# A decoder layer on one Trainium2 core: auxiliary products pinned in VectorE's queue, a head with direct column transposes, and modulation halves added on ScalarE

## The chip, the cores and the metric

The kernel runs on one core of a Trainium2 chip. The metric is the device time of one execution in microseconds, the median of several. The core has a matrix engine (TensorE, PE in the profile, with PEld for its weight loads), VectorE (DVE), ScalarE (ACT), GpSimd (POOL) and a sync engine (SP) that issues nearly all DMAs here. Each engine takes its instructions in the order of its own queue and waits on semaphores for the others.

## The reference

One layer on 256 tokens with 2048 channels, in float32:

```python
mod = silu(c) @ w_mod + b_mod
sh1, sc1, g1, sh2, sc2, g2 = jnp.split(mod, 6, axis=-1)
h = _rms_norm(x, mix_norm_pre) * (1.0 + sc1) + sh1
y = _token_mixer(h, ...)       # h @ w_in, attention, gated linear attention, merge, w_out
x = x + g1 * _rms_norm(y, mix_norm_post)
h = _rms_norm(x, ffn_norm_pre) * (1.0 + sc2) + sh2
y = _conv_ffn(h, ...)          # h @ w_up, conv of width 3, silu(gate) * value, w_down
x = x + g2 * _rms_norm(y, ffn_norm_post)
```

`c` is one vector of 2048 values, `w_mod` has 2048 x 12288 entries; `_rms_norm` divides each token by its root mean square.

## The kernel before

All weights pass through the core once. A weight *item* is 128 rows x 2048 columns, cut into two *parts* of 128 x 1024 (512 KB). Every product keeps float32 accuracy by splitting both operands into a rounded high half and the rest: for a part, ACT casts `hi` from the loaded `raw` (L272), DVE subtracts `lo = raw - hi` (L276), and PE multiplies hi by h_hi, lo by h_hi and hi by h_lo (`mm3`, L292 to L294). In the stages that put 512 columns out, a part is 12 matmuls of 512 columns; in `half_mm` (L343) it is 8 pairs of a 512-column and a 256-column matmul.

The loop at L1175 goes over the parts: at step q SP issues the load of part q+3 (four `raw` buffers), ACT and DVE prepare part q (three `hi`, three `lo` buffers), and PE multiplies part q-3. The stages follow one another: wS (phase 1: attention q, k, v and a quarter of the values), wOG (phase 2: output gate), the forget columns, wQK, wV, wGB and wBB, wGA and wBA, wO, then twice wU and wD.

Beside the weights run 224 *auxiliary* loads of 128 x 1024. For 192 of them DVE makes a product with `cact`, the silu of c copied to all partitions, and sums along the row (`mod_proc`, L207): two halves give one column of `mod`, added up at L211. The other 32 (`bias_proc`, L226) add the shift's share of the attention projection. The first 64 are *early*: they give scale and shift for h, one column of 128 channels for each item of phases 1 and 2, and have four buffers; the rest share three, later two, buffers (`auxb`). `aux_step` (L1165) runs the products that are due by their `pos` and issues the next loads.

The order on PE and SP is that of the code. On DVE and ACT a scheduler sets it, by its own estimate of when operands are there, except in blocks marked `manual_schedule`, such as the head. So an L207 stands in DVE's queue where the scheduler put it.

The head (L131 to L175) builds `cact`: for each 128 values of c DVE scales the identity by them, and PE multiplies it by ones, so that they stand on all partitions (L136, L139); ACT copies them out of PSUM (L143). It also squares x (DVE one half at L147, ACT the other at L149), makes 1/rms, and transposes x by a matmul with a diagonal of 1/rms (L171), whose result ACT copies to `xnT` (L173). `make_h1` (L352) then forms the column factor `a` on DVE (L355), h_hi on ACT (L357) and h_lo on DVE (L358); in phase 2 `make_h2` (L362) overwrites them with the shifted h (L365, L297, L298). `evac_1` (L372) takes phase 1's eight PSUM banks out, those of the first token tile (t = 0) on ACT, those of the second on DVE.

Of the kernel before, what the change touches and what calls it, by code (L numbers as in the profile page):

```python
# [38 lines left out]
def block_kernel(ctx: ExitStack, tc: tile.TileContext, x, cvec, pos, idn, cst, vec, vec2, gmask,  # L39
# [90 lines left out]
    with tc.manual_schedule(engines={ET.DVE, ET.Activation}):  # L130
        nc.scalar.activation(ccol, ccol, AF.Silu)  # L131

        def c_diag(n):
            dg = t2k()
            for j in range(4):
                nc.vector.tensor_scalar(out=dg[:, j * P:(j + 1) * P], in0=ident, scalar1=ccol[:, 4 * n + j:4 * n + j + 1],  # L136
                                        scalar2=None, op0=ALU.mult)
            ps = bank(n)
            nc.tensor.matmul(out=ps, lhsT=ones[:, :P], rhs=dg, start=True, stop=True)  # L139
            return ps  # L140

        def c_copy(n, ps):
            nc.scalar.copy(cact[:, n * 512:(n + 1) * 512], ps)  # L143

        def sums(t):
            ssx = small(2, "ssx")
            nc.vector.scalar_tensor_tensor(out=junk[:, t, :HW], in0=xh[:, t, :HW], scalar=1.0, in1=xh[:, t, :HW],  # L147
                                           op0=ALU.mult, op1=ALU.mult, accum_out=ssx[:, 0:1])
            nc.scalar.activation(junk[:, t, HW:], xh[:, t, HW:], AF.Square, accum_out=ssx[:, 1:2])  # L149
            return ssx  # L150

        def scale(ssx):
            ssy = small(1, "ssy")
            nc.vector.tensor_tensor(ssy, ssx[:, 0:1], ssx[:, 1:2], op=ALU.add)
            return diag_of(rstd_of(ssy, 1, float(D)))

        cps = [c_diag(n) for n in range(3)]
        c_copy(0, cps[0])
        s0 = sums(0)
        cps.append(c_diag(3))  # L160
        c_copy(1, cps[1])
        c_copy(2, cps[2])
        dgs = [scale(s0)]
        s1 = sums(1)
        c_copy(3, cps[3])
        for t in range(2):
            for q in range(4):
                pt = bank((4, 5, 6, 7, 0, 1, 2, 3)[4 * t + q])
                for j in range(4):
                    c = 4 * q + j  # L170
                    nc.tensor.matmul(out=pt[:, j * P:(j + 1) * P], lhsT=xh[:, t, c * P:(c + 1) * P], rhs=dgs[t],  # L171
                                     start=True, stop=True)
                nc.scalar.copy(xnT[:, 4 * q:4 * q + 4, t * P:(t + 1) * P], pt.rearrange("p (c t) -> p c t", c=4))  # L173
# [1111 lines left out]
```

## Time and profile before

| | |
|---|---|
| median of 3 runs | 1598.68 us (1593.1 to 1600.93) |
| profiled execution | 1597.75 us, of which the span from the first to the last instruction is 1595.6 us |
| busy share of PE, DVE, ACT | 98%, 77%, 52% |
| mean granted TensorE clock | 0.997 |
| moved from HBM | 399.68 MB, 252 GB/s over the span |

Busy times are sums of instruction durations over the span; a matmul's end is modelled, so the distance between two starts says more on PE than its busy share. A wait is put down to the instruction that came last by the profile. Times of instructions are microseconds from the start of the span.

### The profile page before, as it was taken

To read this page: it belongs to the slowest core of one execution; us is meant where nothing else is said; L and a number is where in the kernel's file an instruction comes from. 1 tells how busy PE (TensorE), PEld (TensorE's weight loads), DVE (VectorE), ACT (ScalarE), POOL (GpSimd) and SP (SyncE) were. 2 spreads that over 40 slices of the span, in tenths; PEclk is the share of its full clock that TensorE was granted. 3 is DMA by queue.
4 is the path that set the end of the run, shared out by engine and by line. 5 is a ranking of instruction groups with operands and counts; after the bars stand their busy time and mean duration, and the time that the engine had idled before them with its cause. 6 is when DMAs were issued, how large, how long until landed. Compare 5 with 4: busy or idle time off the path is not lost.

```text
span 1595.6 us, 21287 instructions
## 1 busy us (share of the span) xinstructions
PE 1563.3 (98%) x7752; PEld 1293.2 (81%) x7752; DVE 1222.5 (77%) x1869; ACT 825.7 (52%) x1221; POOL 17.0 (1%) x35
## 2 busy tenths in 40 slices
PE   8999999999999999999999999999999999999997
PEld 6878888877767788777888888888778888888886
DVE  7999989968977778877778877777546777776446
ACT  5455565544477544443366555555335555555333
POOL 0000000000000000000000000000000000000001
PEclk9999999999999999999999999999999999999999
DMA  9999987877777799889935667677665555555554
GB/s 367 382 352 410 360 274 257 277 273 256 250 244 263 257 306 326 293 293 314 354 133 199 230 231 238 217 245 231 231 224 187 182 185 185 186 186 189 194 197 132
DMA packets 154841, 403.18 MB, mean 253 GB/s; under 512 B 12720, under 2 KB 70704, under 8 KB 154480
## 3 DMA queue, kind: packets, MB, share of 16 engines
q1 hardware_dynamic: 154736, 401.82, 72.9%
q8 instruction: 61, 1.00, 0.3%
q14 instruction: 44, 0.36, 0.1%
HBM read 399.68 MB, written 2.10 MB: 252 GB/s over the span
## 4 chain that ended last, share of the span: by engine, by line
PE 31%; DMA 22%; DVE 13%; issue 5%; ACT 2%; SPq 1%; POOL 0%; DVEq 0%; POOLq 0%; ACTq 0%
DMA aux<-in_wM_dram 21%; PE ps L343 16%; DVE lo L276 6%; PE ps L293 5%; PE ps L294 5%; PE ps L292 5%; DVE aux L207 2%; DMA raw<-in_wO_dram 1%; ACT hi L272 1%; SPq L251 0%; DVE aux L348 0%; DVE t2k L742 0%; DVE t2k L1093 0%; DVE y L1134 0%; SPq L253 0%
## 5 line engine op out<-in xcount | busy, mean ns | idle before, releaser
L272 ACT CAST hi<-raw 128x1024 fp32r<-128x1024 f32 x520 | 544.9, 1050 | 476.1 <-PE ps L294 366.9
L276 DVE TENSOR_TENSOR lo<-raw,hi 128x1024 fp32r<-128x1024 f32 x518 | 629.2, 1221 | 142.0 <-ACT hi L272 139.6
L343 PE MATMUL ps<-h,hi 128*128 128x512 f32 x1664 | 582.0, 398 | 1.0 <-DVE h L1051 1.0
L343 PE MATMUL ps<-h,lo 128*128 128x256 f32 x1664 | 451.0, 281 | 1.0 <-DVE lo L276 0.9
L343 PEld LDWEIGHTS ps<-h,hi 128*128 128x128 f32 x1664 | 306.4, 188 | 69.2 <-issue 1.3
L343 PEld LDWEIGHTS ps<-h,lo 128*128 128x128 f32 x1664 | 314.0, 189 | 13.8 <-DVE lo L276 4.4
L207 DVE SCALAR_TENSOR_TENSOR aux<-aux,cact 128x1024 f32<-128x1024 f32 x128 | 156.4, 1223 | 145.7 <-DMA aux<-in_wM_dram 145.6
L292 PE MATMUL ps<-hi,h 128*128 128x512 f32 x608 | 240.0, 395 | 1.6 <-ACT h L297 1.1
L293 PE MATMUL ps<-lo,h 128*128 128x512 f32 x608 | 237.4, 391 | 2.6 <-DVE lo L276 2.5
L294 PE MATMUL ps<-hi,h 128*128 128x512 f32 x608 | 237.1, 390 | 1.5 <-DVE h L298 0.8
L293 PEld LDWEIGHTS ps<-lo,h 128*128 128x128 f32 x608 | 114.2, 188 | 29.2 <-DVE lo L276 4.9
L294 PEld LDWEIGHTS ps<-hi,h 128*128 128x128 f32 x608 | 114.1, 188 | 26.9 <-DVE h L298 1.2
L292 PEld LDWEIGHTS ps<-hi,h 128*128 128x128 f32 x608 | 114.2, 188 | 26.7 <-ACT h L297 1.5
L293 PE MATMUL ps<-lo,act_ab 128*128 128x512 f32 x256 | 100.3, 392 | 2.2 <-DVE lo L276 2.2
L294 PE MATMUL ps<-hi,act_ab 128*128 128x512 f32 x256 | 99.7, 389 | 0.0
L292 PE MATMUL ps<-hi,act_ab 128*128 128x512 f32 x256 | 99.7, 389 | 0.0
L207 DVE SCALAR_TENSOR_TENSOR early<-early,cact 128x1024 f32<-128x1024 f32 x64 | 78.0, 1218 | 1.3 <-ACT cact L143 1.3
L347 ACT ACTIVATE aux<-ps 128x256 f32<-128x256 f32 x88 | 33.5, 380 | 75.4 <-PE ps L343 75.2
L1090 ACT ACTIVATE t2k<-aux,vc 128x256 f32<-128x256 f32 x88 | 52.8, 601 | 26.6 <-DVE aux L348 26.4
L348 DVE SCALAR_TENSOR_TENSOR aux<-ps,aux 128x256 f32<-128x256 f32 x88 | 37.0, 421 | 35.6 <-ACT aux L347 35.6
L293 PEld LDWEIGHTS ps<-lo,act_ab 128*128 128x128 f32 x256 | 48.0, 188 | 14.4 <-DVE lo L276 4.6
L292 PEld LDWEIGHTS ps<-hi,act_ab 128*128 128x128 f32 x256 | 48.0, 188 | 10.1
(270 smaller groups left out, 1614.2 us busy)
## 6 DMA issues: line engine op xcount, KB each, us to landing
raw<-in_wU_dram SPq DMA_DIRECT2D x176, 512.0 KB, 3.8
aux<-in_wM_dram SPq DMA_DIRECT2D x128, 512.0 KB, 6.0
raw<-in_wD_dram SPq DMA_DIRECT2D x88, 512.0 KB, 3.9
early<-in_wM_dram SPq DMA_DIRECT2D x64, 512.0 KB, 6.7
raw<-in_wS_dram SPq DMA_DIRECT2D x32, 512.0 KB, 6.4
raw<-in_wOG_dram SPq DMA_DIRECT2D x32, 512.0 KB, 7.0
aux<-in_wS_dram SPq DMA_DIRECT2D x32, 512.0 KB, 5.7
raw<-in_wQK_dram SPq DMA_DIRECT2D x32, 512.0 KB, 5.4
```

The lines of the kernel that those rows point to most:

```text
L207: nc.vector.scalar_tensor_tensor(out=raw, in0=raw, scalar=1.0, in1=cact[:, half * HW:(half + 1) * HW], op0=ALU.mult, op1=ALU.mult, accum_o ...
L272: nc.scalar.copy(hi[:, :w], raw)
L276: nc.vector.tensor_tensor(lo[:, :w], raw, hi[:, :w].bitcast(F32), op=ALU.subtract)
L292: nc.tensor.matmul(out=o, lhsT=lh, rhs=rh, start=start, stop=False)
L293: nc.tensor.matmul(out=o, lhsT=lh, rhs=rl, start=False, stop=False)
L294: nc.tensor.matmul(out=o, lhsT=ll, rhs=rh, start=False, stop=stop)
L343: nc.tensor.matmul(out=o, lhsT=w, rhs=m, start=c == 0 and o is ps, stop=c == nk - 1 and o is ps)
L347: nc.scalar.activation(o, ps[:, TOK:], AF.Copy, scale=scale)
L348: nc.vector.scalar_tensor_tensor(out=o, in0=ps[:, :TOK], scalar=scale, in1=o, op0=ALU.mult, op1=ALU.add)
L1090: nc.scalar.activation(z, u, AF.Identity, scale=w2, bias=vc2[:, W_CB + f:W_CB + f + 1])
```

## The change

Three edits. **Products.** Each auxiliary product after the 64 early ones is traced inside `tc.issue_after(...)`: it gets an ordering edge, without a semaphore, behind the subtraction L276 of part `lq + 3`, where `lq` is the step at which its load was issued. **Head.** `cact` comes from transposing each column of c, broadcast along 128 columns, so DVE's sixteen scaled identities and the ones go; the first token tile is still transposed against the diagonal, the second is scaled by DVE first and transposed against the identity; `vec` is loaded from ACT's queue; parts 0 and 1 are prepared inside the head; the first half item of phase 1 runs its twelve matmuls as four hi, four lo, four h_lo. **Adds.** For the columns of phases 1 and 2, ACT adds each half as it comes (`Identity` with a column as bias, in phase 1 also one as scale) where DVE had one addition at the end and one for the factor; and `evac_1` gives two more of its eight copies to ACT.

```diff
-    nc.sync.dma_start(out=ident, in_=idn)
     nc.sync.dma_start(out=ccol, in_=cvec)
+    nc.sync.dma_start(out=ident, in_=idn)
...
-    nc.sync.dma_start(out=vc, in_=vec)
...
+    nc.scalar.activation(ccol, ccol, AF.Silu)
+    nc.scalar.dma_start(out=vc, in_=vec)
+    for n in range(4):
+        ps = bank((2, 6, 3, 7)[n])
+        for j in range(4):
+            nc.tensor.transpose(ps[:, j * P:(j + 1) * P], ccol[:, 4 * n + j:4 * n + j + 1].to_broadcast([P, P]), ident)
+        cps.append(ps)
...
+    c_copy(0)
+    square_v(0, 0)
+    nc.scalar.activation(junk[:, 0, HW:], xh[:, 0, HW:], AF.Square, accum_out=ssx[0][:, 1:2])
+    for n in range(1, 4):
+        c_copy(n)
+    rs = rstd_x(0)
+    square_v(1, 0)
+    nc.scalar.activation(junk[:, 1, HW:], xh[:, 1, HW:], AF.Square, accum_out=ssx[1][:, 1:2])
+    dg0 = diag_of(rs)
+    rs = rstd_x(1)
+    for q in range(2):
+        xs = xh[:, 1, q * HW:(q + 1) * HW]
+        nc.vector.tensor_scalar(out=xs, in0=xs, scalar1=rs, scalar2=None, op0=ALU.mult)
+    bw = modc[:, 16:32]
+    nc.vector.scalar_tensor_tensor(out=bw, in0=vc[:, V_BMOD + 16:V_BMOD + 32], scalar=1.0,
+                                   in1=vc[:, V_PRE1:V_PRE1 + 16], op0=ALU.add, op1=ALU.mult)
+    def x_transposes(t, qs=range(4)):
...
+                if t == 0:
+                    nc.tensor.matmul(out=pt[:, j * P:(j + 1) * P], lhsT=xc, rhs=dg0, start=True, stop=True)
+                else:
+                    nc.tensor.transpose(pt[:, j * P:(j + 1) * P], xc, ident)
+            nc.scalar.copy(xnT[:, 4 * q:4 * q + 4, t * P:(t + 1) * P], pt.rearrange("p (c t) -> p c t", c=4))
...
+        if idx < 32:
+            c = idx % 16
+            w, b, o = (1.0, vc[:, V_BMOD + c:V_BMOD + c + 1], modc) if idx < 16 else (vc[:, V_PRE1 + c:V_PRE1 + c + 1], bw[:, c:c + 1], acol)
+            o = o[:, c:c + 1]
+            nc.scalar.activation(o, acc[:, half:half + 1], AF.Identity, scale=w, bias=o if half else b)
+            if half:
+                a["post"]()
+            return
...
-        a["raw"] = raw
+        a["raw"], a["lq"] = raw, S.get("q", 0)
...
-        (mod_proc if a["kind"] == "mod" else bias_proc)(a, a["half"], a.pop("raw"))
+        go = mod_proc if a["kind"] == "mod" else bias_proc
+        if i < N_EARLY:
+            return go(a, a["half"], a.pop("raw"))
+        with tc.issue_after(los[max(k for k in los if k <= a["lq"] + LAG)]):
+            go(a, a["half"], a.pop("raw"))
...
-            nc.vector.tensor_tensor(lo[:, :w], raw, hi[:, :w].bitcast(F32), op=ALU.subtract)
+            los[it["q"] + half] = nc.vector.tensor_tensor(lo[:, :w], raw, hi[:, :w].bitcast(F32), op=ALU.subtract).ins
...
+    LAG, los = 3, {}
...
+                for k in range(3):
+                    for n in range(2):
+                        for t in range(2):
...
+                            nc.tensor.matmul(out=S["acc", 4 * t + n], lhsT=(xh_, xh_, xl_)[k](0)[:, t * P:(t + 1) * P],
+                                             rhs=(hi, lo, hi)[k][:, n * 512:(n + 1) * 512], start=k == 0, stop=False)
...
-            nc.vector.scalar_tensor_tensor(out=a, in0=modc[:, 16 + c:17 + c], scalar=1.0,
-                                           in1=vc[:, V_PRE1 + c:V_PRE1 + c + 1], op0=ALU.add, op1=ALU.mult)
...
-        if t == 0:
+        if t == 0 or n < 2:
             nc.scalar.copy(dst, ps)
...
+            elif q == 0:
+                x_transposes(0, range(3))
+                S["lo0"] = prep(*parts[q][:2], defer=True)
+                x_transposes(0, range(3, 4))
+                x_transposes(1, range(1))
+                aux_step(1)
+                lo1 = prep(*parts[1][:2], defer=True)
+                x_transposes(1, range(1, 4))
+                lo1()
+                head.close()
```

DVE's queue in the head, before (L136 are the scaled identities, L147 the squares, L207 the first two early products) and after (L145 the squares, L166 the scaling of the second token tile, L214 the early products, L296 and L391 lo and h_lo):

```order
L136 TENSOR_SCALAR t2k<-ident,ccol 128x128 x12
L147 SCALAR_TENSOR_TENSOR bf_116,ssx<-xh 128x1024
L136 TENSOR_SCALAR t2k<-ident,ccol 128x128 x4
L154 TENSOR_TENSOR ssy<-ssx 128x1
L113 TENSOR_SCALAR ms_156<-ssy 128x1
L120 TENSOR_SCALAR diag<-ident,rs_158 128x128
L147 SCALAR_TENSOR_TENSOR bf_116,ssx<-xh 128x1024
L207 SCALAR_TENSOR_TENSOR early,macc<-early,cact 128x1024
L154 TENSOR_TENSOR ssy<-ssx 128x1
L113 TENSOR_SCALAR ms_192<-ssy 128x1
L120 TENSOR_SCALAR diag<-ident,rs_194 128x128
L207 SCALAR_TENSOR_TENSOR early,macc<-early,cact 128x1024
```

```order
L145 SCALAR_TENSOR_TENSOR bf_113,ssx<-xh 128x1024
L150 TENSOR_TENSOR ssy<-ssx 128x1
L112 TENSOR_SCALAR ms_148<-ssy 128x1
L145 SCALAR_TENSOR_TENSOR bf_113,ssx<-xh 128x1024
L119 TENSOR_SCALAR diag<-ident,rs_150 128x128
L150 TENSOR_TENSOR ssy<-ssx 128x1
L112 TENSOR_SCALAR ms_158<-ssy 128x1
L166 TENSOR_SCALAR xh<-xh,rs_160 128x1024 x2
L170 SCALAR_TENSOR_TENSOR modc<-vc 128x16
L214 SCALAR_TENSOR_TENSOR early,macc<-early,cact 128x1024 x2
L296 TENSOR_TENSOR lo<-raw,hi 128x1024
L214 SCALAR_TENSOR_TENSOR early,macc<-early,cact 128x1024
```

The sixteen small products at the top are gone, two wide multiplications have come, and both early products now follow the whole of x's scaling.

DVE's queue in the first wD stage, around 1110 us, before and after, with buffer numbers (those of after are 7 higher for the same `raw`, `hi` and `lo`; L207 and L214 are the product, L276 and L297 the subtraction):

```order
L276 TENSOR_TENSOR lo_9664<-raw_9607,hi_9663 128x1024
L276 TENSOR_TENSOR lo_9685<-raw_9625,hi_9684 128x1024
L207 SCALAR_TENSOR_TENSOR aux0_102,macc_9799<-aux0_102,cact_113 128x1024
L276 TENSOR_TENSOR lo_9703<-raw_9643,hi_9702 128x1024
L276 TENSOR_TENSOR lo_9721<-raw_9661,hi_9720 128x1024
L276 TENSOR_TENSOR lo_9742<-raw_9682,hi_9741 128x1024
```

```order
L297 TENSOR_TENSOR lo_9671<-raw_9614,hi_9670 128x1024
L297 TENSOR_TENSOR lo_9692<-raw_9632,hi_9691 128x1024
L297 TENSOR_TENSOR lo_9710<-raw_9650,hi_9709 128x1024
L297 TENSOR_TENSOR lo_9728<-raw_9668,hi_9727 128x1024
L214 SCALAR_TENSOR_TENSOR aux0_101,macc_9806<-aux0_101,cact_112 128x1024
L297 TENSOR_TENSOR lo_9749<-raw_9689,hi_9748 128x1024
```

The product stood ahead of lo_9703 and now stands behind lo_9728, the same part's successor: two subtractions later.

ACT's queue at the end of phase 1, before and after (L379 and L412 are `evac_1`'s copies, L221 the adds, L365 and L398 with L297 and L319 the first h of phase 2):

```order
L357 ACTIVATE h_112<-bf1_116,acol_108 128x256
L379 COPY qkv_962<-ps0_266 128x512
L272 CAST hi_955<-raw_871 128x1024
L379 COPY qkv_962<-ps1_274 128x512
L379 COPY qkv_962<-ps2_294 128x512
L272 CAST hi_986<-raw_895 128x1024
L379 COPY vb_963<-ps3_302 128x512
L365 ACTIVATE t2k_927<-bf1_116,modc_107,acol_108 128x256
L297 CAST h_112<-t2k_927 128x256
```

```order
L388 ACTIVATE h_111<-bf1_113,acol_107 128x256
L412 COPY qkv_955<-ps0_258 128x512
L293 CAST hi_948<-raw_863 128x1024
L221 ACTIVATE modc_106<-macc_914,vc_96 128x1
L412 COPY qkv_955<-ps4_260 128x512
L412 COPY qkv_955<-ps1_262 128x512
L412 COPY qkv_955<-ps5_264 128x512
L412 COPY qkv_955<-ps2_285 128x512
L293 CAST hi_979<-raw_886 128x1024
L221 ACTIVATE modc_106<-macc_914,modc_106 128x1
L412 COPY vb_956<-ps3_293 128x512
L398 ACTIVATE t2k_919<-bf1_113,modc_106,acol_107 128x256
```

Two copies (banks ps4 and ps5) and two adds have come in ahead of phase 2's first h.

## Rows read from the trace of the kernel before

**Rows 1.** The page's part 1: engines, busy us (share of the span), instructions.

```profile
PE 1563.3 (98%) x7752; PEld 1293.2 (81%) x7752; DVE 1222.5 (77%) x1869; ACT 825.7 (52%) x1221; POOL 17.0 (1%) x35
```

**Rows 2.** Stretches: us, busy (instructions) of each engine, granted clock, DMA share, GB/s.

```profile
50.00:100.00 50.00, 50.00 (x221) 41.12 (x220) 49.37 (x83) 24.20 (x28) 0.00 (x0) 1.00 1.02 382
...
850.00:1180.00 330.00, 326.88 (x1733) 276.97 (x1733) 242.06 (x368) 170.14 (x248) 0.21 (x1) 1.00 0.69 233
1200.00:1466.00 266.00, 266.00 (x1486) 230.02 (x1485) 192.26 (x277) 150.59 (x232) 0.00 (x0) 1.00 0.56 186
```

**Rows 3.** Waits: engine, tile, line <- releaser: us in total, times, longest.

```profile
DVE aux L207 <- DMA aux<-in_wM_dram: 145.6, 87, 4.5
...
PEld ps L293 <- DVE lo L276: 15.6, 23, 1.8
...
PE ps L293 <- DVE lo L276: 7.4, 12, 1.4
...
PEld ps L343 <- DVE lo L276: 4.4, 10, 0.8
```

**Rows 4.** Timeline, 1112 to 1124 us: start, us, engine, line, operation [idle before <- releaser].

```profile
1112.18 0.43 SPq L239 DMA_DIRECT2D aux<-in_wM_dram  x1
...
1119.07 1.05 ACT L272 CAST hi<-raw 128x1024 fp32r<-128x1024 f32 x1 [1.67 <-PE ps L294]
...
1120.42 1.23 DVE L207 SCALAR_TENSOR_TENSOR aux<-aux,cact 128x1024 f32<-128x1024 f32 x1 [4.49 <-DMA aux<-in_wM_dram]
...
1121.57 3.49 DVE L276 TENSOR_TENSOR lo<-raw,hi 128x1024 fp32r<-128x1024 f32 x3
1121.59 0.39 PE L292 MATMUL ps<-hi,act_ab 128*128 128x512 f32 x1
...
1122.85 0.50 PE L293 MATMUL ps<-lo,act_ab 128*128 128x512 f32 x1 [0.87 <-DVE lo L276]
```

**Rows 5.** Timeline of PE at 417 us.

```profile
417.71 0.50 PE L293 MATMUL ps<-lo,ob 128*128 128x512 f32 x1 [0.90 <-DVE lo L276]
```

**Rows 6.** Timeline of the head, all engines.

```profile
10.41 1.06 ACT L149 ACTIVATE bf<-xh 128x1024 f32<-128x1024 f32 x1
...
14.41 1.22 DVE L207 SCALAR_TENSOR_TENSOR early<-early,cact 128x1024 f32<-128x1024 f32 x1
14.52 1.04 ACT L272 CAST hi<-raw 128x1024 fp32r<-128x1024 f32 x1 [0.20 <-DMA raw<-in_wS_dram]
...
18.91 0.50 PE L292 MATMUL ps<-hi,h 128*128 128x512 f32 x1 [0.51 <-ACT h L357]
...
20.34 0.50 PE L294 MATMUL ps<-hi,h 128*128 128x512 f32 x1 [0.69 <-DVE h L358]
...
22.73 0.39 PE L292 MATMUL ps<-hi,h 128*128 128x512 f32 x1
```

**Rows 7.** Line L224: durations in ns (min/median/max).

```profile
L224 DVE TENSOR_SCALAR bias_v<-aux,modc x2: 747/748/748, 185.9 to 195.7; 128x1024 f32<-128x1024 f32 x2
```

**Rows 8.** Timeline of PE at the end of phase 1.

```profile
107.05 0.39 PE L294 MATMUL ps<-hi,h 128*128 128x512 f32 x1
108.51 0.50 PE L292 MATMUL ps<-hi,h 128*128 128x512 f32 x1 [1.07 <-ACT h L297]
...
110.05 0.50 PE L294 MATMUL ps<-hi,h 128*128 128x512 f32 x1 [0.81 <-DVE h L298]
```

**Rows 9.** ACT's groups by line and form: busy us, mean ns of one.

```profile
L297 ACT CAST act_ab<-t2k 128x256 fp32r<-128x256 f32 x32 | 13.0, 407 | 24.9 <-DVE t2k L1099 24.9
...
L365 ACT ACTIVATE t2k<-bf,modc,acol 128x256 f32<-128x256 f32 x16 | 9.6, 603 | 14.3 <-DVE modc L211 14.3
...
L357 ACT ACTIVATE h<-bf,acol 128x256 fp32r<-128x256 f32 x16 | 8.2, 512 | 3.4 <-DVE acol L355 2.4
...
L379 ACT COPY qkv<-ps 128x512 f32<-128x512 f32 x3 | 1.8, 587 | 2.4 <-PE ps L294 2.4
```

**Rows 10.** DMA issues: tile, count, KB each, median us to landing.

```profile
raw<-in_wO_dram SPq DMA_DIRECT2D x32, 512.0 KB, 6.2
```

More of the change, by code (lines that the diff above doesn't have):

```diff
@@ L129, in block_kernel @@
     junk = bf1[:, 1].rearrange("p (t c) k -> p t (c k)", t=2)
[L130 to L134, printed above, removed]
-            for j in range(4):
[L136 to L173, printed above, removed]
-            if t == 0:
-                dgs.append(scale(s1))
@@ new lines, in block_kernel, with c_copy @@
+    head = ExitStack()
+    head.enter_context(tc.manual_schedule(engines={ET.DVE, ET.Activation}))
+    nc.scalar.activation(ccol, ccol, AF.Silu)
+    nc.scalar.dma_start(out=vc, in_=vec)
+    cps = []
+    for n in range(4):
[3 more added lines that the diff above has]
+        cps.append(ps)
+    ssx = [small(2, "ssx") for _ in range(2)]
+    def c_copy(n):
+        nc.scalar.copy(cact[:, n * 512:(n + 1) * 512], cps[n])
@@ new lines, in square_v, with rstd_x @@
+    def square_v(t, q):
+        xs = xh[:, t, q * HW:(q + 1) * HW]
+        nc.vector.scalar_tensor_tensor(out=junk[:, t, q * HW:(q + 1) * HW], in0=xs, scalar=1.0, in1=xs,
+                                       op0=ALU.mult, op1=ALU.mult, accum_out=ssx[t][:, q:q + 1])
+    def rstd_x(t):
+        ssy = small(1, "ssy")
+        nc.vector.tensor_tensor(ssy, ssx[t][:, 0:1], ssx[t][:, 1:2], op=ALU.add)
+        return rstd_of(ssy, 1, float(D))
+    c_copy(0)
+    square_v(0, 0)
+    nc.scalar.activation(junk[:, 0, HW:], xh[:, 0, HW:], AF.Square, accum_out=ssx[0][:, 1:2])
@@ new lines, in x_transposes @@
+    def x_transposes(t, qs=range(4)):
+        for q in qs:
+            pt = bank((0, 4, 1, 5, 2, 6, 3, 7)[4 * t + q])
+            for j in range(4):
+                xc = xh[:, t, (4 * q + j) * P:(4 * q + j + 1) * P]
+                if t == 0:
[3 more added lines that the diff above has]
+            nc.scalar.copy(xnT[:, 4 * q:4 * q + 4, t * P:(t + 1) * P], pt.rearrange("p (c t) -> p c t", c=4))
@@ L314, in go @@
         def go(it, half, hi, lo):
+            if half == 0 and c == 0 and x_of is h_of and evac is evac_1:
+                xh_, xl_ = x_of()
+                for k in range(3):
+                    for n in range(2):
+                        for t in range(2):
+                            if k == 0:
+                                S["acc", 4 * t + n] = bank(4 * t + n)
+                            nc.tensor.matmul(out=S["acc", 4 * t + n], lhsT=(xh_, xh_, xl_)[k](0)[:, t * P:(t + 1) * P],
+                                             rhs=(hi, lo, hi)[k][:, n * 512:(n + 1) * 512], start=k == 0, stop=False)
+                return
             if not split or c < n_all - 3:
@@ L354, in go @@
             a = acol[:, c:c + 1]
[L355 to L356 removed]
             nc.scalar.activation(h_hi[:, c], xnT[:, c], AF.Copy, scale=a)
+            if c == 0:
+                S["lo0"]()
             nc.vector.scalar_tensor_tensor(out=h_lo[:, c], in0=xnT[:, c], scalar=a, in1=h_hi[:, c].bitcast(F32),
@@ L1157, in block_kernel @@
         nh = -(-it["n"] // HW)
+        it["q"] = len(parts)
         parts += [(it, hf, hf == nh - 1) for hf in range(nh)]
@@ L1175, in block_kernel @@
     for q in range(n + PR):
+        S["q"] = q
         if q >= PR:
@@ L1193, in block_kernel @@
                 loaded += 1
-            if early:
+            if early and q:
                 aux_step(q)
```

5 lines of the change are left out of this document (1 added, 4 removed).

## The prediction

> **What bounds the kernel now.** I read the busy shares first: PE is busy 98% of the span [rows 1]. Matmul ends are modelled, so the stretches come next. From 50 to 100 us PE starts 221 matmuls of 512 columns in 50 us, one every 0.226 us without a pause, and VectorE (DVE) is busy for 49.37 of those 50 us [rows 2]: PE sets the pace and DVE only just keeps up. From 1200 to 1466 us, where no auxiliary product runs, PE is busy for 266.00 of 266.00 us; from 850 to 1180 us, where they run, it loses 3.1 of 330 us even by this generous count [rows 2]. So PE has no slack: a late operand costs the end its full length, and time is to be won only at PE's pauses.
>
> The waits say which operand is late. The weight loads of the matmuls that read `lo` (L293, L343) wait for DVE's subtraction L276 for 15.6 us in 23 pauses and 4.4 us in 10; the L293 matmuls themselves stand idle for 7.4 us in 12 [rows 3]. On DVE the largest wait is that of the auxiliary product L207 for its own DMA, 145.6 us in 87 pauses [rows 3]. The stretch at 1120 us shows how the two belong together: SP issues the product's 512 KB at 1112.18; DVE, an in-order queue, waits for them 4.49 us, multiplies at 1120.42, and only then runs three subtractions back to back; the first of them ends at about 1122.8, and PE, whose hi matmul started at 1121.59, starts the lo matmul at 1122.85, idle for 0.87 us [rows 4].
>
> **Step 1, the pin.** Each auxiliary product from the 65th on is now ordered behind the subtraction of the part three after the one at which its load was issued. The compiled order shows the effect: the product at 1120.42 runs behind two more subtractions than before. ScalarE (ACT) casts one hi per part (12 matmuls, 2.7 us); the second of the two subtractions needs the hi cast at 1119.07 for 1.05 us [rows 4], runs from 1120.2 and ends at about 1121.3. The product's data landed by 1120.42, so no wait is left, and no subtraction stands behind one. The margin, 0.9 us, is thin because this is the longest of the 87 waits; a mean one is 145.6 / 87 = 1.7 us [rows 3] against a shift of two parts, 5.4 us.
>
> What this is worth: the bounds are PE's own idle time before a lo, 7.4 us [rows 3], and all that the weight loads waited, 20.0 us [rows 3]. The idle time is short by what a restart costs: in [rows 4] start to start is 1.26 us where 0.23 is normal, so 1.03 is lost where 0.87 is shown, and the next matmul is late again by about 0.1. Twelve pauses with 0.26 added to each make 7.4 + 3.1 = 10.5 us; the other 21 load waits, (20.0 less about 8.3) / 21 = 0.56 us each, are mostly covered by the matmul before them, and I take 0.15 each, 3.2 us. Of the 13.7 us some have another cause: at 417.71 PE waits 0.90 for a lo that the rotary products hold up, no DMA [rows 5]. I take 1.7 off: **-12.0**, with 6 and 20 as ends. Nearest to it is the stretch without products, where nothing is lost. The product itself, 1.2 us of DVE, is moved and not removed; in the example a part leaves DVE 1.5 us beside one subtraction of 1.2, which covers it.
>
> **Step 2, the head.** Today the squares of the last x chunk run on ACT at 10.41, when it lands; DVE does the second early product at 14.41; raw lands and hi starts at 14.52; the first lo matmul series starts at 18.91, its third matmul waits for h_lo until 20.34, and the second part begins at 22.73 [rows 6]. The new head drops 16 small products on DVE and four wide matmuls, which run while x is still landing and cost nothing; x landing stays the bound until 10.4. From there: ACT's square ends 11.7; sum, scale and power 0.9, so the second token tile is scaled from 12.7. These two 128x1024 multiplications are not in the trace there; the same form takes 0.748 us at L224 [rows 7] (a product of two tensors would be 1.22; I take 0.75). They end at 14.1, the small `bw` at 14.3, the two early products at 16.7, lo at 17.8, a third product at 19.0, h_lo at 19.4. ACT adds the halves at 16.75 and makes h by 17.7. PE starts at 17.75 instead of 18.91. Its new order, four hi, four lo, four h_lo matmuls, spends 1.8 us before it needs h_lo, so it hardly waits: the first half ends at 20.5, where the second part begins, against 22.73. **-2.2**; ends -0.8 (multiplications at 1.22, vc landing late) and -3.2.
>
> **Step 3, ACT's adds.** 64 one-column ACTIVATEs replace 48 tiny DVE instructions. A form of 128x256 costs 0.407 without a pointer operand, 0.512 with one, 0.603 with two [rows 9]; so one column is between 0.2 (the two pointers alone) and 0.6; I take 0.3 and 0.4 for one and two pointers. The Trainium skill ("ScalarE: Activation LUTs", What ACT_TABLE_LOAD costs) gives 186 ns and 93 ns for each pointer operand, by an estimate 0.28 and 0.37 us; the steps of [rows 9], 0.105 and 0.091, agree, and the sum would not change. In phase 1 the second add stands between a hi cast and h: cast 1.05, add 0.4, h 0.51 and some 0.2 of handover are 2.2 us of the 2.7 that a part leaves. Hidden, if it stays so.
>
> At the end of phase 1 it isn't hidden. PE's last matmul starts at 107.05, the next at 108.51 behind ACT's h, the third at 110.05 behind DVE's h_lo [rows 8]. In the new order ACT has two evacuations more (0.587 each [rows 9]) and two adds ahead of that h, so h comes about 1.0 later; DVE has two evacuations less ahead of h_lo, yet must wait for h. Third matmul 0.4 later, and some 0.2 more behind: **+0.6**, ends -0.5 and +2.
>
> **Sum.** 1597.75 for the profiled execution (its span of 1595.6 and 2.15 around it), - 12.0 - 2.2 + 0.6 = 1584.15. The median shown, 1598.68, is 0.93 above that execution: **1585 us**. The measurement tells apart about 0.5%, 8 us: faster is below 1590.7, slower above 1606.7.
>
> **Rivals.** (a) The waits move and half the gain goes. Products stand later, so the buffers they free and the next loads come later too, and some still wait. For it: the 0.9 us margin above. Against: a load now has four parts, 10.9 us, before its product, and the slow one of [rows 4] landed in 8.2. Step 1 at -4 gives 1593.
> (b) It does not do what it says: lo is late because ACT's hi is (as at 417.71, where no DMA is waited for), and h_lo in the head comes no earlier. Then 1598. Against it: the waits stand directly ahead of the late subtractions in [rows 4].
> (c) Slower: SP's queue. It is in order too; a load that waits for its buffer until a later product is done holds the raw loads behind it by up to one product, 1.22 us. Some 128 loads can hold it 156 us; if a fifth reached PE that is 31 us, so 1616. It decides when a raw load has less than 1.22 us to spare. From a subtraction to the hi four parts on are 10.9 us, less 2.4 for cast and subtraction, less 6.2 for a wO load to land [rows 10]: 2.3 to spare where both kinds of load run. Against it, then.
> (d) ACT's adds reach PE in phase 1. If an add takes 0.9 instead of 0.4, h is late by about 0.5 in each of 16 columns: 8 us, 1593. The Trainium skill ("ScalarE: Activation LUTs", Rules for kernel authors) says to put add and mul on VectorE, not on ScalarE; by it this move would be a loss. [rows 2] speak against it here: in this stretch DVE is the full engine.
>
> **How the numbers follow.** Forecast 0.64 (its own range 1579 to 1590), (a) 0.20, (b) 0.05, (c) 0.05, (d) 0.06. Low end: step 1 at its bound of 20 gives 1577. High end: (a) and (d) with the head's poor end, 1597; (b) and (c) stay outside. Faster: the forecast and a little of (a), 0.67; slower: (c), 0.06; same 0.27.
>
> **What would show it.** Right: DVE's wait for the wM DMA falls from 145.6 to under 15 us; the loads' wait for lo from 20.0 to under 6; 850 to 1180 us looks like 1200 to 1466; the first wS matmul at about 17.8, the second part at 20.5; the pause at the end of phase 1 starts 2 us earlier and is no shorter. Wrong: pauses of L293 that remain with no DMA wait ahead of them (b); new waits of hi for raw (c); pauses between 25 and 100 us (d).

## The result and the profile after

The changed kernel takes 1581.69 us (median of 4 runs, 1580.96 to 1581.83) against 1599.81 of the kernel before (1593.1 to 1602.13): a ratio of 0.9893, with a 95% interval of 0.9862 to 0.9923. The profiled execution spans 1578.8 us at a mean granted clock of 0.998, 16.8 less than before. The forecast was 1585, that is 13.6 us less in the profiled execution; the range was 1577 to 1597.

The page's part 1, and of its part 5 the group of the later auxiliary products (busy us, mean ns, then DVE's idle time ahead of them):

```profile
PE 1552.9 (98%) x7744; PEld 1295.6 (82%) x7744; DVE 1219.2 (77%) x1805; ACT 847.2 (54%) x1287; POOL 16.8 (1%) x34
...
L214 DVE SCALAR_TENSOR_TENSOR aux<-aux,cact 128x1024 f32<-128x1024 f32 x128 | 155.7, 1218 | 0.0
```

PE's busy time, which counts the modelled ends of late matmuls too, is 10.4 us below [rows 1]. The 128 products never wait: 0.0 us, where 145.6 stood [rows 3]. The same three stretches as [rows 2]:

```profile
50.00:100.00 50.00, 50.00 (x222) 41.19 (x221) 46.59 (x66) 30.20 (x47) 0.00 (x0) 1.00 1.02 392
850.00:1180.00 330.00, 330.00 (x1743) 282.26 (x1742) 245.25 (x360) 172.00 (x244) 0.20 (x1) 1.00 0.69 233
1200.00:1466.00 266.00, 266.00 (x1484) 229.94 (x1484) 191.42 (x278) 149.89 (x231) 0.00 (x0) 1.00 0.55 185
```

From 850 to 1180 us PE is busy throughout, as from 1200 on. What DVE, ACT and PE wait for now (us in total, times, longest), to be held against [rows 3]:

```profile
DVE lo L297 <- ACT hi L293: 247.4, 301, 4.5
...
ACT hi L293 <- DMA raw<-in_wO_dram: 14.5, 8, 5.2
...
PEld ps L315 <- DVE lo L297: 2.8, 6, 0.7
...
PE ps L315 <- DVE lo L297: 0.6, 3, 0.3
```

DVE now waits for ACT's hi, not for a DMA, and the lo is there in time: the weight loads wait 2.8 us where they waited 15.6, the matmuls 0.6 where it was 7.4. A product of the first wD stage, as in [rows 4]:

```profile
1097.97 0.43 SPq L255 DMA_DIRECT2D aux<-in_wM_dram  x1
...
1108.36 1.22 DVE L214 SCALAR_TENSOR_TENSOR aux<-aux,cact 128x1024 f32<-128x1024 f32 x1
...
1109.94 1.22 DVE L297 TENSOR_TENSOR lo<-raw,hi 128x1024 fp32r<-128x1024 f32 x1 [0.35 <-ACT hi L293]
```

Its load goes out at 1097.97 and DVE takes it up at 1108.36, with no idle time ahead and one subtraction, that of 1109.94, next in line.

Not so in the head. It answers to [rows 6] (PE, DVE and ACT, with the idle time before an instruction and what ended it):

```profile
11.10 1.06 ACT L160 ACTIVATE bf<-xh 128x1024 f32<-128x1024 f32 x1 [1.18 <-DMA xh<-in_x_dram]
11.28 6.04 PE L179 MATMUL ps<-diag,xh 128*128 128x128 f32 x32 [4.24 <-DVE diag L119]
...
13.29 1.42 DVE L166 TENSOR_SCALAR xh<-xh,rs 128x1024 f32<-128x1024 f32 x2 [0.67 <-POOL rs L114]
...
16.46 0.59 ACT L182 COPY bf<-ps 128x512 f32<-128x512 f32 x1 [0.78 <-PE ps L179]
16.94 1.05 ACT L293 CAST hi<-raw 128x1024 fp32r<-128x1024 f32 x1
...
19.28 0.39 ACT L221 ACTIVATE acol<-macc,acol,vc 128x1 f32<-128x1 f32 x1
19.70 0.51 ACT L388 ACTIVATE h<-bf,acol 128x256 fp32r<-128x256 f32 x1
...
20.26 1.20 PE L345 MATMUL ps<-hi,h 128*128 128x512 f32 x4 [1.20 <-ACT h L388]
...
23.11 0.39 PE L314 MATMUL ps<-hi,h 128*128 128x512 f32 x1
```

The last chunk of x comes first: ACT squares it at 11.10, where it did so at 10.41. The first wS matmul starts at 20.26, not 18.91, and the second part at 23.11, not 22.73. PE then pauses twice in phase 1, where before it never did after the first half item, and again at its end, as in [rows 8]:

```profile
31.88 0.49 PE L315 MATMUL ps<-lo,h 128*128 128x512 f32 x1 [0.21 <-DVE lo L297]
...
37.85 0.50 PE L314 MATMUL ps<-hi,h 128*128 128x512 f32 x1 [0.28 <-ACT h L388]
...
108.83 0.39 PE L316 MATMUL ps<-hi,h 128*128 128x512 f32 x1
110.75 0.50 PE L314 MATMUL ps<-hi,h 128*128 128x512 f32 x1 [1.53 <-ACT h L319]
...
111.89 0.50 PE L316 MATMUL ps<-hi,h 128*128 128x512 f32 x1 [0.41 <-DVE h L320]
```

Where the time came from, by the starts of stages on PE's timeline (us; e1_pin, e8_444 and e11_nofill are told below):

| first matmul of | before | after | e1_pin | e8_444 | e11_nofill |
|---|---|---|---|---|---|
| phase 1 | 18.91 | 20.26 | 18.90 | 19.05 | 18.99 |
| its second part | 22.73 | 23.11 | 22.73 | 21.92 | 21.86 |
| (last of phase 1) | 107.05 | 108.83 | 107.16 | 106.46 | 106.35 |
| wV | 303.20 | 305.68 | 305.05 | 302.26 | 302.15 |
| wBB (reads tile `ob`) | 410.98 | 411.05 | 410.43 | 407.63 | 407.53 |
| first wU | 839.69 | 828.41 | 827.21 | 825.06 | 821.82 |
| first wD | 1091.64 | 1078.72 | 1077.53 | 1075.49 | 1072.15 |
| second wU | 1215.30 | 1198.41 | 1197.22 | 1195.18 | 1191.84 |
| (last matmul) | 1585.31 | 1568.42 | 1567.23 | 1565.19 | 1561.85 |

So the change loses 2.48 us up to wV and wins 19.37 behind it, all of it before the second wU, where the products end.

### The profile page after: what moved, and what is told of

Same layout as the page of the kernel before. It is cut to its first block, busy times and chain, and to the rows that moved or that the text cites. A ratio compares the mean times of both kernels' runs of the same rounds, so it can differ in the third digit from the quotient of the medians.

```text
span 1578.8 us, 21309 instructions
## 1 busy us (share of the span) xinstructions
PE 1552.9 (98%) x7744; PEld 1295.6 (82%) x7744; DVE 1219.2 (77%) x1805; ACT 847.2 (54%) x1287; POOL 16.8 (1%) x34
## 4 chain that ended last, share of the span: by engine, by line
PE 67%; DVE 4%; DMA 1%; ACT 1%; issue 1%; POOL 0%; DVEq 0%; POOLq 0%; ACTq 0%
PE ps L376 31%; PE ps L314 11%; PE ps L315 11%; PE ps L316 11%; DMA raw<-in_wO_dram 1%; DVE lo L297 1%; PE ps L769 0%; ACT hi L293 0%; DMA raw<-in_wU_dram 0%; PE ps L816 0%; DVE y L1167 0%; ACT aux L1035 0%; PE ps L802 0%; PE ps L1060 0%; DVE aux L214 0%
## 5 line engine op out<-in xcount | busy, mean ns | idle before, releaser
L297 DVE TENSOR_TENSOR lo<-raw,hi 128x1024 fp32r<-128x1024 f32 x516 | 630.5, 1224 | 251.3 <-ACT hi L293 247.4
L214 DVE SCALAR_TENSOR_TENSOR aux<-aux,cact 128x1024 f32<-128x1024 f32 x128 | 155.7, 1218 | 0.0
L214 DVE SCALAR_TENSOR_TENSOR early<-early,cact 128x1024 f32<-128x1024 f32 x64 | 77.7, 1219 | 0.3 <-DMA early<-in_wM_dram 0.3
L316 PEld LDWEIGHTS ps<-hi,act_ab 128*128 128x128 f32 x256 | 48.0, 188 | 10.0
L314 PEld LDWEIGHTS ps<-hi,act_ab 128*128 128x128 f32 x256 | 48.0, 188 | 9.9
```

The costliest lines, as they stand in the source:

```text
L214: nc.vector.scalar_tensor_tensor(out=raw, in0=raw, scalar=1.0, in1=cact[:, half * HW:(half + 1) * HW], op0=ALU.mult, op1=ALU.mult, accum_o ...
L297: los[it["q"] + half] = nc.vector.tensor_tensor(lo[:, :w], raw, hi[:, :w].bitcast(F32), op=ALU.subtract).ins
L314: nc.tensor.matmul(out=o, lhsT=lh, rhs=rh, start=start, stop=False)
L316: nc.tensor.matmul(out=o, lhsT=ll, rhs=rh, start=False, stop=stop)
```

## The experiments

The kernels ran in three groups of four, each with the kernel before beside it: medians 1606.1, 1603.9 and 1605.1. That kernel's executions scatter over 8 to 18 us within a group, those of the pinned kernels over 0.2 to 2.5 (lag 6 apart), so I compare pinned kernels with each other by their medians, within a group where they differ by little.

### One part at a time

**e1_pin**: the kernel before and the pin alone.

```diff
-        (mod_proc if a["kind"] == "mod" else bias_proc)(a, a["half"], a.pop("raw"))
+        with tc.issue_after(los[max(k for k in los if k <= a["lq"] + LAG)]):
+            go(a, a["half"], a.pop("raw"))
```

> The kernel before with the pin alone; head, ACT's adds and evac_1 stay as before. In the two traces the distance from the first matmul of the third stage (at 200.5 us before, 202.9 after) to the last matmul is 19.3 us shorter after. Theory A: all of that is the pin, so this kernel takes about 19 us off the kernel before, 1580.5, and its stages up to 200 us start where those of before start. Theory B: the pin is worth the 12 us forecast for it, and the head or the adds shorten something later: 1588. Under both, DVE's wait for the wM loads, 145.6 us before, is under 15 us.

1579.0 us, 0.9831 (0.9796 to 0.9867). Theory A: the pin is the whole gain. From wV to the last matmul it takes 1262.2 us, against 1282.1 before and 1262.7 in the changed kernel. Up to 110 us the starts are those of before, within 0.2. Then comes something that I had not expected. The columns are those of [rows 2]; the last but two is the granted clock:

```profile
108.00:110.00 2.00, 0.73 (x2) 0.30 (x2) 2.00 (x4) 1.48 (x3) 0.00 (x0) 1.00 0.88 287
110.00:112.00 2.00, 1.84 (x6) 1.45 (x7) 2.00 (x4) 0.00 (x0) 0.00 (x0) 0.70 1.04 270
112.00:114.00 2.00, 2.00 (x6) 1.59 (x5) 2.00 (x5) 0.25 (x1) 0.00 (x0) 0.50 0.93 285
```

Behind the two pauses at 107 to 110 us, which stand in the kernel before too [rows 8], the granted clock falls to 0.5, that is 1.2 of 2.4 GHz, and some nine matmuls start up to 0.2 us later each, 1.6 in all. That is why wV starts late here too. The two longer of its four executions, 1579.68 (the profiled one) and 1579.97, have a mean granted clock of 0.997, the two shorter, 1577.71 and 1578.34, of 0.998.

**e2_nopin**: the changed kernel without the pin.

```diff
-        with tc.issue_after(los[max(k for k in los if k <= a["lq"] + LAG)]):
-            go(a, a["half"], a.pop("raw"))
+        go(a, a["half"], a.pop("raw"))
```

> The changed kernel without the pin: products are traced with no ordering edge. Theory A (the pin alone brings the gain; head and adds cost 2.4 us by 200 us): about 2.4 us above the kernel before, 1602, and DVE's wait for the wM loads is back at over 100 us. Theory B (head -2.2 and boundary +0.6 as forecast): 1.6 below it, 1598.

1609.1 us, 1.0013 (0.9992 to 1.0035) of the kernel before. The waits are back:

```profile
DVE aux L214 <- DMA aux<-in_wM_dram: 148.0, 86, 4.8
...
PE ps L314 <- DVE lo L296: 11.0, 15, 1.6
```

Head and adds by themselves bring nothing that can be measured; the interval holds theory A's +2.4 us and not a gain of 1.6.

**e3_noadds**: the changed kernel without ACT's adds and with `evac_1` as before.

```diff
-        if idx < 32:
...
-            nc.scalar.activation(o, acc[:, half:half + 1], AF.Identity, scale=w, bias=o if half else b)
...
-        if t == 0 or n < 2:
+        if t == 0:
```

> The changed kernel with the additions of the halves and the factor back on DVE and evac_1's eight copies split four to four as before; pin and new head stay. Theory A: ACT's adds cost the pauses at 31 and 37 us (0.4 each at least, with restarts 1.2 in all), and the end of phase 1 is as long either way (2.4 before, 2.5 after): 1 us below the changed kernel, 1580.7. Theory B: the pauses at 31 and 37 us are DVE catching up after a late head, whoever adds; with 48 small instructions back, about 0.2 each, DVE is later still: 0 to 2 us above the changed kernel, 1582 to 1584.

1580.1 us; the changed kernel itself, run again as **e5_after** in the second group, 1580.3.

> The changed kernel itself, unaltered, beside the others of this group, since differences of 1 to 3 us are in question. 1581.7 as before; DVE never waits for the wM loads of the later products.

Neither theory holds alone. The pause at 31 us goes with the adds, two at 36 and 37 us stay (0.33 and 0.27 us idle), and the clock falls to 0.5 at 112. The medians put the adds at about nothing. But the profiled execution of e3_noadds has that fall in it, and its two executions with a mean clock of 0.998 took 1579.3 us: that the adds cost up to 1 us is not excluded.

### The head

**e4_warm**: the changed kernel with PE kept busy while x lands.

```diff
     c_copy(0)
+    warm = bank(5)
+    for _ in range(5):
+        nc.tensor.matmul(out=warm[:, :256], lhsT=ident, rhs=cact[:, :256], start=True, stop=True)
```

> The changed kernel with five matmuls of 256 columns on PE between the transposes of c and those of x; their result is read by nobody. In the changed kernel PE stands idle from 7.0 to 11.3 us and then takes about 0.18 us for each of the first 32 transposing matmuls, against 0.114 in the kernel before, where wide matmuls ran up to 10.9 us. Theory A: the pause ahead makes them slow; with it filled they take 0.114, the last of them ends about 2 us earlier, h comes 1.5 to 2 us earlier, the second part starts at about 21.3 instead of 23.1, and the time is 1.5 to 2.5 below the changed kernel, 1579.5. Theory B: they are slow for another reason (operand layout, PSUM banks, loads of weights): pace 0.18 stays, and the time is that of the changed kernel, 1581.7, or later by what the added matmuls delay.

PE's timeline (L156 are the added matmuls, L182 the transposes of the first token tile, L348 and L317 the wS matmuls):

```profile
6.82 2.95 PE L156 MATMUL ps<-cact,ident 128*128 128x256 f32 x10
...
11.11 3.84 PE L182 MATMUL ps<-diag,xh 128*128 128x128 f32 x32 [1.35 <-DVE diag L119]
...
18.06 1.19 PE L348 MATMUL ps<-hi,h 128*128 128x512 f32 x4 [1.36 <-ACT h L391]
...
20.91 0.39 PE L317 MATMUL ps<-hi,h 128*128 128x512 f32 x1
```

Theory A for the pace. Without the filling, 32 transposing matmuls took 6.04 us; behind five filling matmuls they take 3.84. The stretch from 11 to 14 us, of the changed kernel, of e4_warm, and of e5_after, the changed kernel run again (PE's records: 12, 25 and 11; the last number but two is the granted clock):

```profile
11.00:14.00 3.00, 2.72 (x12) 2.72 (x13) 1.24 (x7) 1.74 (x3) 0.55 (x1) 1.00 1.03 422
```

```profile
11.00:14.00 3.00, 2.89 (x25) 2.89 (x26) 1.27 (x5) 2.23 (x4) 0.56 (x1) 1.00 1.03 421
```

```profile
11.00:14.00 3.00, 2.46 (x11) 2.46 (x12) 1.27 (x6) 1.50 (x3) 0.55 (x1) 0.51 1.02 419
```

The 1.00 of the first row is no reading: that trace has no entry of the clock before 15.92 us, and a stretch without an entry counts as 1.00. Its transposes start every 0.213 us up to 15.71 and every 0.112 from 15.92 on. In e5_after, the same kernel, the entries reach further back: the clock is 0.5, that is 1.2 of 2.4 GHz, from 11.04 to 14.46, and the transposes start every 0.213 us up to 14.26 and every 0.112 from 14.47 on. In e4_warm it is 1.00 from 8.07 on, and they start every 0.112 from 11.33 on, as those of the kernel before do (1.00 from 10.39 on). The edit changed only what PE did in the 4.2 us before: behind that pause the clock is low, behind the filling it is not. The Trainium skill ("TensorE: Matmul & The Clock Gate", What's actually happening) has the array throttled by default until activity releases it; e5_after's 0.51 and e4_warm's 1.00 agree.

When the clock rises differs from execution to execution, and the first wS matmul moves with it: 14.46 and 19.70 us in e5_after, 15.92 and 20.26 in the changed kernel's first trace, 16.09 and 20.40 in e12_less. With the filling the second part starts at 20.91, 2.2 us earlier than in that first trace and 1.6 earlier than in e5_after (22.55). But the median, 1580.25, is that of e5_after: phase 1 then lasts 0.6 us longer than the changed kernel's, with pauses at 29 and 35 us, and at 110 the clock falls.

So what does phase 1 cost once it runs? From the start of its second part to its last matmul:

| kernel | second part | to the last | head, adds |
|---|---|---|---|
| before, e1_pin, e8_444, e11_nofill | 22.73, 22.73, 21.92, 21.86 | 84.3, 84.4, 84.5, 84.5 | old, DVE |
| after, e5_after, e12_less | 23.11, 22.55, 23.25 | 85.7, 85.8, 85.8 | new, ACT |
| e4_warm | 20.91 | 86.4 | new, ACT |
| e3_noadds, e9_all | 22.65, 21.16 | 85.9, 86.4 | new, DVE |

31 parts at 2.72 us are 84.3. Every kernel with the new head pays 1.4 to 2.1 more, whoever adds; none with the old head does, though e8_444 and e11_nofill start 0.8 earlier.

**e12_less**: four products of DVE cut short.

```diff
+        w = 256 if idx in (17, 18) else HW
-        nc.vector.scalar_tensor_tensor(out=raw, in0=raw, scalar=1.0, in1=cact[:, half * HW:(half + 1) * HW],
+        nc.vector.scalar_tensor_tensor(out=raw[:, :w], in0=raw[:, :w], scalar=1.0, in1=cact[:, half * HW:half * HW + w],
```

> The changed kernel with the four products of the second and third column of scale (idx 17 and 18) over 256 of their 1024 columns, so that these two columns of the result's scale are left incomplete; it takes about 0.85 us off DVE for each, 3.4 us in all, between 19 and 35 us, and changes no load. In the changed kernel PE starts its second part no later than in the kernel with the pin alone, yet pauses at 31 and 37 us. Theory A (DVE enters phase 1 some 3 us behind what it had done in the old head, and at 49 of 50 us busy can't catch up): both pauses go, and the time is 1.0 to 1.3 us below the changed kernel beside the second group, 1579.1. Theory B (ACT's adds delay h and hi): the pauses stay, 1580.3.

1580.7 us, no gain: theory A falls as I put it. The pause at 31 us is gone, the one at 37 has grown, and it now follows a hi that waited for its raw load:

```profile
35.77 1.05 ACT L294 CAST hi<-raw 128x1024 fp32r<-128x1024 f32 x1 [1.82 <-DMA raw<-in_wS_dram]
...
37.70 0.50 PE L315 MATMUL ps<-hi,h 128*128 128x512 f32 x1 [0.51 <-ACT h L389]
```

So it is not DVE's work alone. The loads of the weights are late too. SP's fifth and sixth go out right behind the first two subtractions, which free their buffers: at 17.38 and 18.90 in e8_444 (the sixth is shown), at 19.28 and 22.44 in the changed kernel (one row for both):

```profile
18.90 0.33 SPq L257 DMA_DIRECT2D raw<-in_wS_dram  x1
```

```profile
19.28 3.49 SPq L274 DMA_DIRECT2D raw<-in_wS_dram  x2
```

The sixth goes out at 20.74 in e4_warm, 21.45 in e9_all and 22.58 in e12_less, against 18.75 to 18.90 with the old head. In the new head's order the second hi is cast only behind the first h of phase 1, at 20.11 in the changed kernel, where it was at 16.43 before. That phase 1 loses its time by these late loads fits the waits, but was not tried.

### How far behind to pin

**e6_lag2** and **e7_lag6**: the changed kernel with `LAG, los = 2, {}` and `6, {}`.

> The changed kernel with each product pinned one part earlier (lag 2 instead of 3); in the compiled order the products then stand one part later than in the kernel before, not two. Of the 87 waits of the kernel before (145.6 us) 14 are longer than one part of 2.73 us, by 10.8 us together. Theory A (the waits are only shifted, so the shift must cover the longest): about 10 us of waiting for wM remain on DVE, a third to a half of it reaches PE, 3 to 5 us above the changed kernel, 1585 to 1587. Theory B (an order free of the long waits also draws the loads forward, so one part suffices): under 3 us of waiting, and the time of the changed kernel, 1581.7.

> The changed kernel with the products pinned three parts later still where code order allows (lag 6 instead of 3); in the compiled order they then stand on average some three parts, 8 us, later than in the kernel before, against two in the changed kernel. Theory A (later products cost nothing, DVE has room wherever it stands): 1580.3, as the changed kernel beside the second group. Theory C (SP, in order, holds the raw loads behind a load that waits for its buffer): SP's wait for the products, 38 us in 34 waits in the changed kernel, grows several times over, ACT's hi waits for raw loads, and the time is 5 to 30 us longer, 1585 to 1610.

Lag 2: 1578.0 us, 2.3 below e5_after. I had taken the longest waits as what has to be covered; one part's shift leaves almost nothing of them:

```profile
DVE aux L214 <- DMA aux<-in_wM_dram: 1.7, 3, 0.9
```

and the time differs above all at one place, the softmax at 465 us (1.93 us on PE's timeline). Before, a product that waited 3.30 us for its DMA stood ahead of two small DVE steps (the second is L757) that ACT's softmax (L760) needs, and PE waited for ACT's copy of the transposed result (timeline of before, all engines, then PE):

```profile
467.04 1.22 DVE L207 SCALAR_TENSOR_TENSOR aux<-aux,cact 128x1024 f32<-128x1024 f32 x1 [3.30 <-DMA aux<-in_wM_dram]
...
468.66 1.70 ACT L760 ACTIVATE t2k<-t2k,dn 128x256 f32<-128x256 f32 x4 [1.50 <-DVE dn L757]
...
470.27 0.56 ACT L772 COPY t2k<-ps 128x512 f32<-128x512 f32 x1
...
470.88 1.71 PE L783 MATMUL ps<-t2k,qkv 128*64 128x512 f32 x2 [2.38 <-ACT t2k L772]
```

In the changed kernel (e5_after) 0.86 us of that are left; with lag 2 ACT's queue has one step of the rotary tables (L867) behind the softmax instead of ahead of it, and between 456 and 466 us one table load of 1.28 us instead of three, and the four matmuls run through:

```profile
467.56 1.07 PE L816 MATMUL ps<-t2k,qkv 128*64 128x512 f32 x2 [0.86 <-ACT t2k L805]
```

```profile
465.31 1.08 PE L816 MATMUL ps<-t2k,qkv 128*64 128x512 f32 x4
```

Lag 6: 1588.3 us, 0.9890 (0.9835 to 0.9945). SP, with the load in its own queue, waits for the products; the first row is of e5_after, the fence below of e7_lag6 (with ACT's wait for wO):

```profile
SPq L255 <- DVE aux L214: 37.8, 34, 4.2
```

```profile
SPq L255 <- DVE aux L214: 202.8, 68, 8.3
SPq L255 <- DVE bias_v L242: 82.8, 24, 7.0
SPq L255 <- DVE modc L227: 82.3, 28, 7.5
...
ACT hi L293 <- DMA raw<-in_wO_dram: 21.0, 7, 7.8
```

That is rival (c) of the prediction, met at lag 6: of the 10.4 us by which its last matmul comes later than e5_after's, 7.0 are lost between wO's first matmul and the first wU, where I had found 2.3 us to spare. Of these 7.0, 1.6 are a fall of the granted clock to 0.50 from 760.6 to 764.0 us, behind two pauses of PE; another fall, behind the end of phase 1, is part of the other 3.4.

### The end of phase 1

**e8_444**: the kernel before, the pin, the first half items of phases 1 and 2 in the new order, and five matmuls that fill the pause ahead of phase 2.

```diff
+            if half == 0 and c == 0 and x_of is h_of:
+                for k in range(3):
+                    for n in range(2):
+                        for t in range(2):
...
+                                if n == t == 0 and evac is not evac_1:
+                                    for _ in range(5):
+                                        nc.tensor.matmul(out=S["acc", 0], lhsT=h_hi[:, 15, :P], rhs=hx[:, 15].rearrange("p s t -> p (s t)"), start=True, stop=True)
+                            nc.tensor.matmul(out=S["acc", 4 * t + n], lhsT=(xh_, xh_, xl_)[k](0)[:, t * P:(t + 1) * P],
+                                             rhs=(hi, lo, hi)[k][:, n * 512:(n + 1) * 512], start=k == 0, stop=False)
+                return
```

> The kernel before with the pin, and with the first half item of phases 1 and 2 run as four hi, four lo, four h_lo matmuls; ahead of phase 2's, five matmuls of 512 columns with a result that nobody reads fill PE's pause. In the kernel with the pin alone PE pauses 1.23 and 0.98 us at 107 to 110 us, and in the profiled execution its granted clock is then 0.5 for some 3 us, which costs 1.76 us; the four timed executions lie 1.7 us apart in two pairs, as if it fell in every second. Theory A (the fall follows the pause, and in phase 1 DVE, busy 49 of 50 us, gives nothing back for an earlier start): no clock fall, the second of the two pauses gone, the 1.1 us won at the first half item lost again as pauses before 100 us: 1577. Theory B (the earlier start stays): 1576. Theory C (the fall has another cause): it is still there, 1578 to 1580.

1577.6 us, 1.4 below e1_pin (of another group) and within 0.2 in all four executions. Theory A comes nearest in time, but not by its sum: of the 0.8 us won in the first half item 0.7 are still there at the end of phase 1, and of the pause ahead of h_lo, 0.98, the next h gives 0.66 back at 113 us. **e9_all** has the new head, warm, with the adds on DVE and the same boundary:

> The changed kernel with its PE kept busy ahead of the transposes of x, with the additions and evac_1's copies back on DVE, and with the first half item of phase 2 run as four hi, four lo, four h_lo behind five filling matmuls. If the parts simply add: 1581.7, less 2.2 at the start of phase 1 of which DVE gives back 1 to 2, less 1.0 at the end of phase 1 and 1 for the adds, no clock fall: 1578. If instead DVE alone sets phase 1, it is as e8_444, 1577, since both end phase 1 when DVE does.

1577.8 us, between its two accounts, and neither holds: it starts its second part 0.8 earlier than e8_444 and ends phase 1 1.1 later, so DVE's work, which is the same in both from there on, doesn't set the end alone.

**e10_lag2** is e8_444 with lag 2, **e11_nofill** that without the filling (`range(0)`).

> The kernel of the second group that ran fastest (old head, the pin, the first half items of phases 1 and 2 as four hi, four lo, four h_lo, five filling matmuls; 1577.6) with lag 2 instead of 3. With lag 2 the changed kernel was 2.3 us faster, all of it at one place: at 461 to 468 us ACT made the softmax some 2.7 us earlier and PE's pause of 0.86 us before the product with it was gone. Theory A (that is an order on ACT which follows from the lag): the same 2.2 us here, 1575.4. Theory B (the order fell so by chance in that kernel alone): 1577.6.

> The kernel e10_lag2 without the five filling matmuls. Theory A (the pause at 106 to 108 us brings the clock down afterwards): in some executions the granted clock is 0.5 for some 3 us after 110, 1.7 us more; the median lies 0 to 1.7 above e10_lag2 and the executions spread as far. Theory B (one pause of 1.2 us, with the second one gone, is too little for it, so the fillers do nothing): the time of e10_lag2, all four within 0.4.

1575.2 and 1574.9 us, 0.9809 (0.9746 to 0.9872) and 0.9808 (0.9756 to 0.9861) of the kernel before, and about 5 us below the changed kernel: the fastest here. Theory A for the lag, theory B for the filling, which does nothing that shows, though the four of e11_nofill lie within 1.05 us and not within 0.4. PE in e11_nofill, and its windows row at 110:

```profile
107.78 1.20 PE L331 MATMUL ps<-hi,h 128*128 128x512 f32 x4 [1.04 <-ACT h L303]
108.81 1.08 PE L331 MATMUL ps<-lo,h 128*128 128x512 f32 x4
109.73 1.08 PE L331 MATMUL ps<-hi,h 128*128 128x512 f32 x4
...
110.00:112.00 2.00, 2.00 (x10) 1.66 (x9) 2.00 (x4) 0.00 (x0) 0.00 (x0) 1.00 1.03 250
```

The pause ahead of h stays; the one ahead of h_lo is gone, and the clock holds.

## Why the prediction was right, and where it was not

The time lay in the range and 3.3 us below the forecast, but the terms are further off than their sum.

**The pin: -12.0 forecast, -19.4 between the two traces, near the upper end of 6 to 20.** Beside each other the medians of the kernel before and e1_pin lie 27.1 us apart, beyond that end: the execution whose waits I read, 1597.75, is among the faster ones of a kernel that takes 1593.1 to 1614.9. The mechanism is as told, and it shows in 0.0 us of waiting. The pauses around the matmuls that read lo, which I summed, shrink by 13.4 us from wV on (start to start on PE's timeline, less 0.227 us a matmul). What I left out are the other readers of DVE behind a waiting product: 3.1 us at the softmax (13.35 us from 461.77 before, 10.23 after), and some 3 in steps of a few tenths at other stage ends. Of the 3.1, 1.5 are the shorter pause itself. The other 1.6 are the granted clock, 0.50 in the kernel before behind that pause and 1.00 in the changed kernel:

```profile
471.20:474.60 3.40, 3.40 (x12) 1.58 (x12) 3.00 (x4) 2.94 (x5) 0.00 (x0) 0.50 0.12 26
```

The step that failed is "all that the weight loads waited" as a bound: it took lo for the only operand that is late, and it left the clock out. The 1.7 us that I took off for pauses with another cause were in part won as well: the one at 417.71, my example, is gone (1.06 us, of which 0.32 comes back 6 us later).

**The head: -2.2 forecast, +0.4 measured** at the second part, and -0.2 in e5_after. The two scalings came as worked out, 1.42 us against 1.5. The step that failed is "four wide matmuls, which run while x is still landing and cost nothing". Behind them the granted clock was at 1.00 when the transposes began; without them it was at 0.5 wherever the trace has an entry. With filling matmuls in their place PE starts at 18.06 and the second part at 20.91, where I had 17.75 and 20.5. "x landing stays the bound until 10.4" failed by 0.7 us: its last chunk landed at 11.08, and at 10.87 to 11.31 in all nine traces with the new head, against 10.39 to 10.59 in the five with the old one. That the load of `vec`, which now lands at about 8 us instead of 10.7, pushes it back is likely and was not tried. The next step failed too: an earlier start was to last to the end, and with the new head phase 1 itself is 1.4 us longer.

**The adds: +0.6 forecast at the end of phase 1.** From the last matmul of phase 1 to the third of phase 2 it was 3.00 us [rows 8] and is 3.06. I had h 1.0 later and the third matmul 0.4; h came 0.46 later and the third matmul, with two copies less ahead of h_lo, 0.06. Another 0.6 is lost in phase 2. An add takes 0.39 us with two pointer operands and 0.29 with one (0.4 and 0.3 forecast). Rival (d), adds that delay h and hi in phase 1, is met at most once, in the pause at 31 us, 0.5 us, not 8; that pause goes without the adds, but with shorter products (e12_less) as well.

**The rivals.** (a) put its weight on a margin of 0.9 us; lag 2 shows that half the shift would do. (b) falls by e1_pin. (c) is real and begins between lag 3 and lag 6. The high end of the range, (a) and (d) with the head's poor end, comes to 1602 by the prices that I gave, not to 1597. The signs I named came true for the pin (waits under 15 and 6 us, 850 to 1180 us without loss) and false for the head (17.8 and 20.5) and the end of phase 1, which was to begin 2 us earlier and begins 1.8 later.

So the forecast was near by luck, because two errors met: 7.4 us too little for the pin, and 4.1 too much hoped for up to wV (-1.6 forecast, +2.48 measured).

## What to carry to other kernels

In an in-order queue an instruction that waits for a DMA delays everything behind it: when it is moved behind later work, count every reader of that engine, not only the one with the longest list of waits, and try one step less and more, since a later consumer frees its buffer later and blocks the queue that loads it. Work that seems useless on the matrix engine may be what keeps its clock up for the work that follows, and a pause there can cost more than its length. Before a granted clock of 1.00 is believed, see whether the trace has an entry for that stretch. An earlier start is worth only what the next stage, with each of its engines and loads full, can keep.

## What the runs showed of the hardware

Transposing matmuls started every 0.213 us at a granted clock of 0.5 and every 0.112 at 1.00 (e5_after). In the head the clock was at 0.5 behind some 4 us without a matmul, in each of the four traces whose entries reach back so far (e3_noadds, e5_after, e6_lag2, e7_lag6), and at 1.00 behind filling work (e4_warm, e9_all).

Two pauses at the end of phase 1, some 1.9 us of idleness together, were followed, in the profiled executions of e1_pin, e3_noadds, e4_warm and e7_lag6, by some 3 us at a granted clock of 0.5, and were not in those of before, after, e2_nopin, e5_after, e6_lag2 and e12_less. With the second pause gone and the first filled (e8_444, e9_all, e10_lag2) or left (e11_nofill) no fall was seen. Behind the softmax's longer pause, of 2.38 and 2.19 us, it fell in both traces without the pin (before, e2_nopin) and in none with it. What decides it is open.

The kernel before scatters over 8 to 18 us, and so does e2_nopin, without the pin (1603.0 to 1612.0); those with it at lag 2 or 3 stay within 2.5. That the scatter comes of DVE's queue following the landing of each load fits this, but is not shown: each unpinned kernel has one trace.
